# Raw weights as single blocks in one ring of six, pooled tiles in the same ring, and the sixth pair of gates ahead of the first `w_pool` products

## The chip, the core and the metric

The kernel runs on one core of one Trainium2 chip. The core has a matrix engine (TensorE, PE in the profile), a vector engine (VectorE, DVE), a scalar engine (ScalarE, ACT), GpSimd (POOL) and an engine that only issues transfers (SyncE, SP); each works through its own list of instructions in order, and they wait for each other by semaphores. The metric is the device time of one execution in microseconds, as the median of several runs.

## What is computed

One layer of a hybrid block on 1024 tokens of width 1024, in float32. Cut to what matters here:

```python
proj = x @ w_in                    # q | f | i | og | pool_v | gate_a | gate_b
a = hgrn2(q, f, i)                 # 8 heads, per-head RMS norm, * sigmoid(og)
a = a @ w_a
b = per_group(causal_mean(pool_v) - pool_v) @ w_pool[g] * pool_scale   # 4 groups
mix = (sigmoid(gate_a) * a + sigmoid(gate_b) * b) @ w_out
x = LN(alpha * x + mix)
x = LN(alpha * x + square(relu(x @ w_up)) @ w_down)
```

## The kernel before

**Precision and products.** Every float32 operand is split into a high and a low part (`split`, L116: a cast on ScalarE, L118, and a subtraction on VectorE, L119), and a product is three passes on TensorE: high by high (L201), high by low (L203), low by high (L204). One product (`prod`) runs over four blocks of 128 rows and so has twelve matmuls of 128x512 into one PSUM bank. Most matrix products are done in Winograd's form: a pair (`pair`, L263) takes four blocks of weights b11, b12, b21, b22 (512 rows by 128 columns each, for two columns of the output) and makes seven products p1 to p7 instead of eight. Between them it needs differences of blocks on VectorE (t1 to t4), copies of a bank out of PSUM (ScalarE, L271), and additions to those copies (VectorE, L275). p1, p6, p5 and p3 go one after the other onto one bank `a`, p7 and p4 onto `z`, p2 onto `c`; each next product on a bank has to wait until the last result has been copied or added.

**What follows what.** After the first matrix products (values of all heads) eight heads follow, with two halves of 512 tokens each (`hgrn`). Behind a half head come other pairs, as `EXTRAS` says: pooled groups, pairs of gates (`gates(0)` to `gates(7)`, called the first to eighth pair), sums of head outputs (`o_sums`), and the products with `w_pool` (`pool_products(g)`, L105 to L107). At the end of each half head stand the output matmuls (L915, L918), their squares on ScalarE (L923), a load of another activation table, a root (L924), a reciprocal on VectorE (L925), four scalings (L928), four transposes on TensorE (L931). The gates' sigmoid (L696) needs the other activation table again. Then come the pairs of `w_a`, `w_out` and the first norm, sixteen pairs of `w_up` (`units`), and `w_down`.

**The order.** The program is written in this order with some priorities (`tc.high_priority`); a scheduler then makes each engine's list from it with its own model of time, and the pools' rings decide which tile waits for whose release. TensorE takes its list in order, and so do ScalarE, VectorE and the transfers' queue on SP: an instruction that waits holds all behind it on the same engine.

**Raw weights.** `raw_tile` (L206) holds two blocks side by side (b11 and b12, or b21 and b22), from a ring of two; `w_blocks` (L209) loads a pair's blocks with two transfers of 512 KB where its two columns lie side by side, and with four of 256 KB otherwise. The differences t have a ring of two of their own (`w_diff`, L239). Pairs that run alone take their products in the order p1, p2, p6, p7, p5, p4, p3; two pairs that run interleaved (`twin`) in the order p1, p2, p7, p4, p6, p5, p3. The pairs of `w_up` take turns between the ring of two and two tiles of another pool.

**Products with `w_pool`.** `pool_products` (L708) loads `w_pool[g]` into a raw tile and splits it into the rings `q` and `f`; the pooled tiles (`pod`, two for each half of the tokens) are loaded into the rings `og`, `v`, `q`, `f` in turn, which the heads use too, and split into the ring `w` of ten tiles. The gates' results that they are multiplied with (L729) are loaded into the same four rings.

Of the kernel before, what the change touches and what calls it, by code (L numbers as in the profile page):

```python
# [16 lines left out]
P = 128  # L17
# [15 lines left out]
PRIO = 60  # L33
# [10 lines left out]
def tile_hybrid_block(  # L44
# [160 lines left out]

    def raw_tile():  # L206
        return wq.tile([P, CH, 2, P], F32, tag="raw", name=nm("raw"), bufs=2)

    def w_blocks(src, c1, c2, tile_of=raw_tile):  # L209

        raw = tile_of(), tile_of()

        def load(*which):
            for kh in range(2):
                rows_of = src[kh * HALF : (kh + 1) * HALF, :].rearrange("(k p) c -> p k c", p=P)
                if c2 == c1 + P and len(which) == 2:
                    done = nc.sync.dma_start(
                        out=raw[kh].rearrange("p k n c -> p k (n c)"), in_=rows_of[:, :, c1 : c1 + 2 * P]
                    )
                else:  # L220
                    for n in which:
                        c = (c1, c2)[n]
                        done = nc.sync.dma_start(out=raw[kh][:, :, n], in_=rows_of[:, :, c : c + P])
            return done

        return raw, load

    def loaded_blocks(*args):
        raw, load = w_blocks(*args)
        load(0, 1)  # L230
        return raw

# [29 lines left out]

    def pair(raw, rooms, takes, pz_tag="pj", twin=False, pc_tag="pj"):  # L263


        b11, b12, b21, b22 = raw if len(raw) == 4 else (raw[kh][:, :, n] for kh in range(2) for n in range(2))
        c, ps = {}, {}
# [46 lines left out]
        def p6(w):  # L314
            prod(ps["a"], w, "s2", False)
            with tc.high_priority(PRIO):
                c[21] = copied(rooms[1], ps["a"])
                if twin:
                    takes[2](added(c[21], ps["z"]))

        def p4(w):
            prod(ps["z"], w, "a22", False)
            if not twin:
                with tc.high_priority(PRIO):
                    takes[2](added(c[21], ps["z"]))

# [75 lines left out]
    with tc.tile_pool(name="xr", bufs=8, side="right", reuse_waits="tile") as xr:  # L402
# [42 lines left out]
        def raw_tile_rows():  # L445
            return [raw_tile().rearrange("p k n c -> p (k n c)").rearrange("p (k c) -> p k c", c=HALF) for _ in range(2)]

# [137 lines left out]
    def raw_rows(src, k2, cc):  # L585

        raw = raw_tile().rearrange("p k n c -> p (k n c)").rearrange("p (k c) -> p k c", c=HALF)
        rows_of = src[k2 * P : (k2 + 2) * P, cc * HALF : (cc + 1) * HALF].rearrange("(k p) c -> p k c", p=P)
        nc.sync.dma_start(out=raw, in_=rows_of)
        return raw  # L590
# [27 lines left out]
    with tc.tile_pool(name="tmp", bufs=1, side="right", reuse_waits="tile") as tmp:  # L618
# [89 lines left out]
        def pool_products(g):  # L708
# [97 lines left out]
        def hgrn(h, u, ft, q, v, og, state):  # L806
# [138 lines left out]
        nxt = head_inputs(0, (None, None, "p6", None, None))  # L945
        output_gates(0)
# [54 lines left out]
        def a_pair(p):  # L1001
            raw = loaded_blocks(w_a, 2 * p * P, (2 * p + 1) * P, raw_tile if p % 2 else mg_raw)
            room = mg_tile("room", 4)
            takes = [gated(2 * p + i, u, p < 2) for u in range(2) for i in range(2)]
            return pair(raw, (c_tile, room, room), takes, "hg", True)

# [75 lines left out]
    with tc.tile_pool(name="wo", bufs=1, side="right", reuse_waits="tile") as mp:  # L1082
        st1 = [None] * 8
        g1, b1 = ln_params(lambda: f(act_tile()).rearrange("p a b -> p (a b)"), ln1_g, ln1_b)
        for k2 in range(0, KT, 2):
            raw = raw_rows(w_out, k2, 1)
            for k in range(2):
                n = len(wo)
                out_row(raw[:, k], (
                    (lambda: (row_tile(), row_tile())) if n < 10 else  # L1090
# [45 lines left out]
    with tc.tile_pool(name="up", bufs=1, side="right", reuse_waits="tile") as up:  # L1136
# [15 lines left out]
        def units(i, raw):  # L1152
# [27 lines left out]

            return pair(raw, (c_tile,) * 3, (take(0), last, take(2), take(3)), "hg", i < 2, "tr" if i == 2 else "pj")

        def up_blocks(i):
            return w_blocks(w_up, i * 2 * P, i * 2 * P + P, up_raw_tile if i % 2 else raw_tile)

        blocks = [up_blocks(i) for i in range(2)]
        for _, load in blocks:
            load(0, 1)
        pairs = [units(i, raw) for i, (raw, _) in enumerate(blocks)]
        run(pairs[0][1:2])  # L1190
# [20 lines left out]
        for i in range(3, NP):  # L1211
            raw, load = up_blocks(i)
            w_load = load(0, 1)
            if i == NP - 2:
                for part in down_rows(0, ws0):
                    part(w_load)
            run(units(i, raw))
# [184 lines left out]
```

## Time and profile before

| | us |
|---|---|
| median of three runs | 1461.98 (1461.56 to 1463.47) |
| the profiled execution | 1460.19 |
| its span, first to last instruction | 1458.5 |
| TensorE busy | 1436.4 |
| VectorE busy | 1141.6 |
| ScalarE busy | 758.3 |

The times in the profile are those of one execution. "Busy" is the union of an engine's instructions; "idle before" is the time that an engine stood ahead of an instruction, with what ended it behind an arrow. Lines (L123) are those of the kernel; tiles are named output first (`w<-raw` is a split of raw weights). A group with `x12` has twelve instructions. The granted clock is the share of full speed at which TensorE was clocked.

### The profile page before, as it was taken

The numbers are of one execution on the slowest core, as the hardware profiler recorded it, in microseconds if no ns is written. First come the engines' busy times: TensorE is split into PE (matmuls) and PEld (weight loads), VectorE is DVE, ScalarE is ACT, GpSimd is POOL, SyncE is SP. The second block draws the span as 40 slices with busy tenths as digits, with TensorE's granted clock in tenths as the row PEclk, the third lists the DMA queues.
The fourth block names the chain that finished last, engine by engine and source line by source line (L and its number), as shares of the span: only waits on it lengthen the run. The fifth ranks groups of instructions, "written<-read, shape, count | busy, mean of one in ns | idle before, by whom it ended". The sixth has DMA issues, their size and how long they took to land.

```text
span 1458.5 us, 20662 instructions
## 1 busy us (share of the span) xinstructions
PE 1436.4 (98%) x7377; PEld 1187.9 (81%) x7377; DVE 1141.6 (78%) x1838; ACT 758.3 (52%) x1383; POOL 58.6 (4%) x244
## 2 busy tenths in 40 slices
PE   8999999999999998999999999999999999999997
PEld 7888888888888886788888878888888888888886
DVE  5967989899898885768985597666666787777977
ACT  5445565666656655556542376555555443333535
POOL 0001001001000010000002100000000100000000
PEclk9999999999999999999999999999999999999999
DMA  7232233323234447897672225444474874445322
GB/s 253 70 126 87 85 98 101 109 75 114 90 99 138 152 132 249 301 299 241 223 247 99 73 94 195 159 146 144 152 261 149 275 260 150 153 141 163 130 73 116
DMA packets 160615, 226.82 MB, mean 156 GB/s; under 512 B 11232, under 2 KB 84480, under 8 KB 160512
## 3 DMA queue, kind: packets, MB, share of 16 engines
q1 hardware_dynamic: 158576, 218.93, 44.7%
q0 software_dynamic: 1152, 4.19, 0.8%
q10 hardware_dynamic: 784, 2.38, 0.5%
q8 instruction: 58, 0.95, 0.3%
q14 instruction: 45, 0.37, 0.1%
HBM read 154.16 MB, written 71.30 MB: 155 GB/s over the span
## 4 chain that ended last, share of the span: by engine, by line
PE 94%; DVE 3%; DMA 1%; ACT 1%; issue 0%; SPq 0%; DVEq 0%
PE ps_pj L201 16%; PE ps_pj L203 16%; PE ps_pj L204 16%; PE ps_pj L1283 4%; PE ps_pj L1285 4%; PE ps_pj L1284 4%; PE ps_pj L106 3%; PE ps_pj L107 3%; PE ps_pj L105 2%; PE ps_tr L1285 1%; PE ps_tr L1283 1%; PE ps_tr L1284 1%; PE ps_sc L201 1%; PE ps_sc L203 1%; PE ps_sc L204 1%; PE ps_hg L203 1%
## 5 line engine op out<-in xcount | busy, mean ns | idle before, releaser
L201 PE MATMUL ps_pj<-act,w 128*128 128x512 f32 x1068 | 421.6, 395 | 0.4 <-ACT act L123 0.2
L203 PE MATMUL ps_pj<-act,w 128*128 128x512 f32 x1068 | 415.1, 390 | 0.5 <-DVE act L124 0.5
L204 PE MATMUL ps_pj<-act,w 128*128 128x512 f32 x1068 | 414.1, 390 | 0.0
L201 PEld LDWEIGHTS ps_pj<-act,w 128*128 128x128 f32 x1068 | 200.6, 188 | 42.8 <-ACT act L123 0.6
L204 PEld LDWEIGHTS ps_pj<-act,w 128*128 128x128 f32 x1068 | 200.5, 188 | 42.3
L203 PEld LDWEIGHTS ps_pj<-act,w 128*128 128x128 f32 x1068 | 200.6, 188 | 40.6 <-DVE act L124 0.9
L118 ACT CAST w<-t 128x512 fp32r<-128x512 f32 x170 | 104.7, 620 | 105.0 <-PE ps_pj L203 53.8
L118 ACT CAST w<-raw 128x512 fp32r<-128x512 f32 x143 | 88.2, 620 | 117.3 <-PE ps_pj L203 62.5
L119 DVE TENSOR_TENSOR w<-raw,w 128x512 fp32r<-128x512 f32 x143 | 99.8, 702 | 55.2 <-ACT w L118 53.9
L119 DVE TENSOR_TENSOR w<-t,w 128x512 fp32r<-128x512 f32 x170 | 115.9, 685 | 29.6 <-ACT w L118 29.4
L1245 ACT CAST act<-act 128x1024 fp32r<-128x1024 f32 x66 | 66.9, 1050 | 107.9 <-issue 35.0
L1246 DVE TENSOR_TENSOR act<-act,act 128x1024 fp32r<-128x1024 f32 x66 | 79.3, 1220 | 18.5 <-ACT act L1245 15.8
L1285 PE MATMUL ps_pj<-act,act 128*128 128x512 f32 x240 | 92.9, 389 | 0.0
L1284 PE MATMUL ps_pj<-act,act 128*128 128x512 f32 x240 | 92.9, 389 | 0.0
L1283 PE MATMUL ps_pj<-act,act 128*128 128x512 f32 x240 | 92.4, 389 | 0.0
L275 DVE TENSOR_TENSOR c<-c,ps_pj 128x512 f32<-128x512 f32 x95 | 64.5, 681 | 18.0 <-PE ps_pj L204 13.4
L271 ACT COPY c<-ps_pj 128x512 f32<-128x512 f32 x96 | 55.2, 582 | 12.8 <-PE ps_pj L204 12.8
L817 DVE RECIPROCAL tC<-tA 128x128 f32<-128x128 f32 x64 | 54.1, 904 | 0.0
L1284 PEld LDWEIGHTS ps_pj<-act,act 128*128 128x128 f32 x240 | 45.1, 188 | 9.4
L1285 PEld LDWEIGHTS ps_pj<-act,act 128*128 128x128 f32 x240 | 45.1, 188 | 9.4
L1283 PEld LDWEIGHTS ps_pj<-act,act 128*128 128x128 f32 x240 | 45.1, 188 | 9.3
L241 DVE TENSOR_TENSOR t<-raw,raw 128x512 f32<-128x512 f32 x43 | 29.6, 689 | 21.9 <-DMA raw<-in_w_in_dram 19.7
(415 smaller groups left out, 2719.8 us busy)
## 6 DMA issues: line engine op xcount, KB each, us to landing
h<-c SPq DMA_DIRECT2D x106, 256.0 KB, 2.1
act<-h SPq DMA_DIRECT2D x78, 256.0 KB, 2.9
raw<-in_w_in_dram SPq DMA_DIRECT2D x64, 256.0 KB, 3.4
draw<-in_w_down_dram SPq DMA_DIRECT2D x16, 1024.0 KB, 7.8
raw<-in_w_up_dram SPq DMA_DIRECT2D x30, 512.0 KB, 4.2
raw<-in_w_in_dram SPq DMA_DIRECT2D x18, 512.0 KB, 4.0
hf<-h SPq DMA_DIRECT2D x34, 256.0 KB, 2.9
c<-o SPq DMA_DIRECT2D x24, 256.0 KB, 3.4
```

What stands on the lines that cost most here:

```text
L118: A.copy(hi, src)
L119: V.tensor_sub(lo, src, f(hi))
L201: PE.matmul(ps, wh[:, k], th, start=first and k == 0, stop=False, skip_group_check=True)
L203: PE.matmul(ps, wh[:, k], tl, start=False, stop=False, skip_group_check=True)
L204: PE.matmul(ps, wl[:, k], th, start=False, stop=k == CH - 1, skip_group_check=True)
L271: A.copy(t, ps)
L275: V.tensor_add(t, t, ps)
L1245: A.copy(hi, src)
L1246: V.tensor_sub(lo, src, f(hi))
L1283: PE.matmul(ps, hh[:, w], wh, start=fresh and n == 0, stop=False, skip_group_check=True)
L1284: PE.matmul(ps, hh[:, w], wl, start=False, stop=False, skip_group_check=True)
L1285: PE.matmul(ps, hl[:, w], wh, start=False, stop=n == M - 1, skip_group_check=True)
```

## The change

Raw weights become single blocks of 128 x 512 (2 KB in each partition) in one ring of six tiles, which also holds the difference t. A pair alone takes five of them, in the order b11, b21, b12, t, b22, each loaded by its own transfer of 256 KB; pairs whose tiles come from another pool keep two wide transfers. All pairs have the product order p1, p2, p7, p4, p6, p5, p3, and the differences are made in place (b12 becomes t1's operand, b21 t4's). The pooled tiles for `w_pool` are loaded into the ring of six. In `EXTRAS` the sixth pair of gates stands ahead of the first products with `w_pool`. The `w_up` pairs from the fourth on all use the ring.

```diff
-    def raw_tile():
-        return wq.tile([P, CH, 2, P], F32, tag="raw", name=nm("raw"), bufs=2)
...
+    def block_tile(shape=(CH, P)):
+        return wq.tile([P, *shape], F32, tag="raw", name=nm("raw"), bufs=6)
+
+    def wide_block(src, kh, c, t):
+        rows_of = src[kh * HALF : (kh + 1) * HALF, :].rearrange("(k p) c -> p k c", p=P)
+        done = nc.sync.dma_start(out=t, in_=rows_of[:, :, c : c + t.shape[2]])
+        return t, done
+
+    def wide_blocks(src, c1, tile_of):
+        raw = [wide_block(src, kh, c1, tile_of().rearrange("p k n c -> p k (n c)"))[0] for kh in range(2)]
+        return [raw[kh][:, :, n * P : (n + 1) * P] for kh in range(2) for n in range(2)]
+
+    def loaded_blocks(src, c1, c2, done=None):
+        raw = {}
+        for i in ((0, 0), (1, 0), (0, 1), "t", (1, 1)):
+            raw[i] = block_tile(), None
+            if i != "t":
+                raw[i] = wide_block(src, i[0], (c1, c2)[i[1]], raw[i][0])
+        if done is not None:
+            done.append(raw[1, 1][1])
+        return [raw[i][0] for i in ((0, 0), (0, 1), (1, 0), (1, 1), "t")]
...
-    def w_diff(a, b):
-        t = wq.tile([P, CH, P], F32, tag="t", name=nm("t"), bufs=2)
-        V.tensor_sub(t, a, b)
-        return t
...
         def t3():
-            c["t"] = w_diff(b22, b12)
+            c["t"] = block_tile() if t is None else t
+            V.tensor_sub(c["t"], b22, b12)
             return w_part(c["t"])
-        def t2():
-            if not twin:
-                V.tensor_add(c["t"], c["t"], b11)
-            return w_part(c["t"])
-
         def t4():
-            if not twin:
-                V.tensor_sub(c["t"], b21, c["t"])
-                return w_part(c["t"])
-            V.tensor_add(c["t"], c["t"], b11)
+            V.tensor_sub(b12, b12, b11)
+            V.tensor_sub(c["t"], b22, b12)
             V.tensor_sub(b21, b21, c["t"])
             return w_part(b21)
+        def t2():
+            return w_part(c["t"])
+
         def t1():
-            return w_part(w_diff(b12, b11))
+            return w_part(b12)
...
-        return (
-            ((t0,), ((t0, p1),)),
-            ((b_21,), ((b_21, p2),)),
-            *(
-                (((t3,), ((t3, p7),)), ((t4,), ((t4, p4),)), ((t2,), ((t2, p6),)), ((t1,), ((t1, p5),)))
-                if twin
-                else (((t3, t2), ((t2, p6), (t3, p7))), ((t1, t4), ((t1, p5), (t4, p4))))
-            ),
-            ((b_22,), ((b_22, p3),)),
+        return tuple(
+            ((operand,), ((operand, product),))
+            for operand, product in ((t0, p1), (b_21, p2), (t3, p7), (t4, p4), (t2, p6), (t1, p5), (b_22, p3))
         )
...
-            raw = raw_tile().rearrange("p k n c -> p (k n c)")[:, : 2 * 2 * P].rearrange("p (k c) -> p k c", c=2 * P)
+            raw = block_tile((2, 2 * P))
             nc.sync.dma_start(out=raw, in_=w_pool[g].rearrange("(k p) c -> p k c", p=P))
...
-                pl = [split(loaded(pod[2 * g + i][u], room), row_tile) for i in range(2)]
+                pl = [split(loaded(pod[2 * g + i][u], lambda: block_tile((HALF,))), row_tile) for i in range(2)]
...
         EXTRAS[7, 1] = (
-            ("gates", 4), ("o_sums", 2), ("pool_products", 0), ("gates", 5), ("pool_products", 1), ("gates", 6), ("pool_products", 2), ("pool_products", 3), ("gates", 7),
+            ("gates", 4), ("o_sums", 2), ("gates", 5), ("pool_products", 0), ("pool_products", 1), ("gates", 6),
+            ("pool_products", 2), ("pool_products", 3), ("gates", 7),
         )
...
-            raw = loaded_blocks(w_a, 2 * p * P, (2 * p + 1) * P, raw_tile if p % 2 else mg_raw)
+            cols = 2 * p * P, (2 * p + 1) * P
+            raw = loaded_blocks(w_a, *cols) if p % 2 else wide_blocks(w_a, cols[0], mg_raw)
...
-        blocks = [up_blocks(i) for i in range(2)]
-        for _, load in blocks:
-            load(0, 1)
-        pairs = [units(i, raw) for i, (raw, _) in enumerate(blocks)]
+        blocks = loaded_blocks(w_up, 0, P), wide_blocks(w_up, 2 * P, up_raw_tile)
+        pairs = [units(i, raw) for i, raw in enumerate(blocks)]
...
         for i in range(3, NP):
-            raw, load = up_blocks(i)
-            w_load = load(0, 1)
+            done = []
+            raw = loaded_blocks(w_up, i * 2 * P, i * 2 * P + P, done)
```

The places that load rows of `x`'s values and of `w_out` through the ring (`raw_tile_rows`, `raw_rows`) take one tile for each row block instead of half a tile.

More of the change, by code (lines that the diff above doesn't have):

```diff
@@ L261, in c_late, with pair @@
         return c_tile(False)
-    def pair(raw, rooms, takes, pz_tag="pj", twin=False, pc_tag="pj"):
-        b11, b12, b21, b22 = raw if len(raw) == 4 else (raw[kh][:, :, n] for kh in range(2) for n in range(2))
+    def pair(raw, rooms, takes, pz_tag="pj", pc_tag="pj"):
+        b11, b12, b21, b22, t = raw if len(raw) == 5 else (*raw, None)
         c, ps = {}, {}
@@ L317, in p6 @@
                 c[21] = copied(rooms[1], ps["a"])
-                if twin:
-                    takes[2](added(c[21], ps["z"]))
+                takes[2](added(c[21], ps["z"]))
         def p4(w):
             prod(ps["z"], w, "a22", False)
-            if not twin:
-                with tc.high_priority(PRIO):
-                    takes[2](added(c[21], ps["z"]))
         def p5(w):
@@ L445, in raw_tile_rows @@
         def raw_tile_rows():
-            return [raw_tile().rearrange("p k n c -> p (k n c)").rearrange("p (k c) -> p k c", c=HALF) for _ in range(2)]
+            return [block_tile((1, HALF)) for _ in range(4)]
         def load_block(tiles, kh, nh, ks=None):
@@ L585, in raw_rows @@
     def raw_rows(src, k2, cc):
-        raw = raw_tile().rearrange("p k n c -> p (k n c)").rearrange("p (k c) -> p k c", c=HALF)
-        rows_of = src[k2 * P : (k2 + 2) * P, cc * HALF : (cc + 1) * HALF].rearrange("(k p) c -> p k c", p=P)
-        nc.sync.dma_start(out=raw, in_=rows_of)
+        raw = [block_tile((HALF,)) for _ in range(2)]
+        for k in range(2):
+            nc.sync.dma_start(out=raw[k], in_=src[(k2 + k) * P : (k2 + k + 1) * P, cc * HALF : (cc + 1) * HALF])
         return raw
@@ L1001, in a_pair @@
         def a_pair(p):
-            raw = loaded_blocks(w_a, 2 * p * P, (2 * p + 1) * P, raw_tile if p % 2 else mg_raw)
+            cols = 2 * p * P, (2 * p + 1) * P
+            raw = loaded_blocks(w_a, *cols) if p % 2 else wide_blocks(w_a, cols[0], mg_raw)
             room = mg_tile("room", 4)
             takes = [gated(2 * p + i, u, p < 2) for u in range(2) for i in range(2)]
-            return pair(raw, (c_tile, room, room), takes, "hg", True)
+            return pair(raw, (c_tile, room, room), takes, "hg")
         def unpark(*which):
@@ L1179, in last @@
                 put(6, s4)
-            return pair(raw, (c_tile,) * 3, (take(0), last, take(2), take(3)), "hg", i < 2, "tr" if i == 2 else "pj")
-        def up_blocks(i):
-            return w_blocks(w_up, i * 2 * P, i * 2 * P + P, up_raw_tile if i % 2 else raw_tile)
-        blocks = [up_blocks(i) for i in range(2)]
-        for _, load in blocks:
-            load(0, 1)
-        pairs = [units(i, raw) for i, (raw, _) in enumerate(blocks)]
+            return pair(raw, (c_tile,) * 3, (take(0), last, take(2), take(3)), "hg", "tr" if i == 2 else "pj")
+        blocks = loaded_blocks(w_up, 0, P), wide_blocks(w_up, 2 * P, up_raw_tile)
+        pairs = [units(i, raw) for i, raw in enumerate(blocks)]
         run(pairs[0][1:2])
```

24 lines of the change are left out of this document (3 added, 21 removed).

## The prediction

> **What bounds the kernel now.** I read the page first, then what TensorE waited for, then the windows around the largest wait, then the order of time on TensorE and ScalarE there, and last how long the loads take to land.
>
> ```profile
> span 1458.5 us, 20662 instructions
> PE 1436.4 (98%) x7377; PEld 1187.9 (81%) x7377; DVE 1141.6 (78%) x1838; ACT 758.3 (52%) x1383; POOL 58.6 (4%) x244
> PE 94%; DVE 3%; DMA 1%; ACT 1%; issue 0%; SPq 0%; DVEq 0%
> ```
>
> TensorE is busy for 98% of the span and makes 94% of the chain that ended last. The number of its products does not change, so an edit counts only by the stretches in which TensorE stands still or is clocked down. What it waited for:
>
> ```profile
> PE ps_pj L105 <- ACT w L118: 4.7, 1, 4.7
> PE ps_hg L915 <- DVE st L883: 1.2, 1, 1.2
> PE ps_pj L106 <- DVE w L119: 0.8, 1, 0.8
> PE ps_sc L201 <- ACT c L271: 0.5, 1, 0.5
> ```
>
> The first three lie within 20 us, where the last head ends and the first products of `w_pool` (L105, L106) begin. Windows over that place (columns: the window, busy us and count of TensorE, its weight loads, VectorE, ScalarE and GpSimd, then the granted clock, the DMA share and GB/s) and over the rest of the kernel behind it:
>
> ```profile
> 574.98:578.40 3.42, 2.05 (x16) 1.86 (x16) 1.72 (x4) 0.12 (x1) 0.00 (x0) 1.00 0.93 280
> 578.40:581.81 3.41, 0.00 (x0) 0.00 (x0) 1.44 (x3) 1.03 (x8) 0.00 (x0) 1.00 0.93 321
> 581.81:588.64 6.83, 5.75 (x13) 3.92 (x14) 2.69 (x5) 5.99 (x13) 0.00 (x0) 0.50 0.67 217
> 600.00:868.00 268.00, 267.17 (x1206) 220.07 (x1205) 205.13 (x334) 127.17 (x222) 14.78 (x6) 1.00 0.59 198
> 868.00:1050.00 182.00, 181.48 (x801) 150.01 (x800) 122.84 (x190) 106.63 (x182) 0.00 (x0) 1.00 0.46 155
> ```
>
> After 3.4 us without one product the clock stands at half for 6.83 us. In these TensorE works 5.75 us at half speed, which loses 5.75 / 2 = 2.9 us. So this place costs 4.7 + 1.2 + 0.8 + 2.9 = 9.6 us. The last two rows lose about a microsecond in 450. Hence a gain is bounded by some 10 us, and all else can only lose.
>
> **The pace of the parts.** One row after the other on TensorE, and the releaser of the long wait on ScalarE:
>
> ```profile
> 559.97 0.39 PE L201 MATMUL ps_pj<-act,w 128*128 128x512 f32 x1
> 560.20 0.39 PE L203 MATMUL ps_pj<-act,w 128*128 128x512 f32 x1
> ...
> 576.14 0.49 PE L915 MATMUL ps_hg<-v,att 128*128 128x128 f32 x2 [1.21 <-DVE st L883]
> 577.80 0.39 PE L918 MATMUL ps_hg<-st,tA 128*128 128x128 f32 x2
> 582.85 1.22 PE L105 MATMUL ps_pj<-w,q 128*128 128x512 f32 x2 [4.66 <-ACT w L118]
> ```
> ```profile
> 554.06 0.62 ACT L118 CAST q<-raw 128x512 fp32r<-128x512 f32 x1 [3.38 <-DMA raw<-in_w_pool_dram]
> 565.13 0.28 ACT L923 ACTIVATE tH<-ps_hg 128x128 f32<-128x128 f32 x1 [0.93 <-PE ps_hg L918]
> 566.29 1.28 ACT L924 ACT_TABLE_LOAD   x1
> 567.59 0.30 ACT L924 ACTIVATE ss<-ss,eps_rms 128x4 f32<-128x4 f32 x1
> 569.99 1.14 ACT L928 ACTIVATE tH<-ps_hg,ss 128x128 f32<-128x128 f32 x4 [2.10 <-DVE ss L925]
> 571.15 1.28 ACT L696 ACT_TABLE_LOAD   x1
> 574.30 0.60 ACT L696 ACTIVATE c<-ps_pj 128x512 f32<-128x512 f32 x1 [0.33 <-PE ps_pj L204]
> 582.18 0.62 ACT L118 CAST w<-og 128x512 fp32r<-128x512 f32 x1 [2.75 <-DMA og<-po]
> ```
>
> A 128x512 matmul goes every 0.227 us, a product of twelve takes 2.72 us; the eight output matmuls of a half head take 576.14 to 578.0, 1.9 us (seven take 1.5). The squares, table load and root of a half head stand from 565.13 to 567.9, 2.8 us; four scalings take 1.14. The long wait ended with a pooled tile's cast: its load into the `og` ring was late.
>
> **The pooled tiles in the raw ring.** They no longer wait for `og` and `v`, which the last head holds. In the order of the changed kernel's instructions their loads stand behind the splits of the sixth pair, well ahead of their casts. That removes the 4.7 us wait, its half clock and the 0.8.
>
> **The sixth pair ahead.** Its p1, p2 and p7 now lie in the end of the last head; p7 and the preceding product cover the 1.2 us wait at L915. Its loads move ahead on SP's queue, and the loads of `w_pool` fall behind them: `w_pool[0]` waits for the split of the fifth pair's last block, `w_pool[1]` for that of b12 of the sixth. On ScalarE, which works in order, the cast of `w_pool[0]` stands ahead of the squares of the last head's first half, the cast of `w_pool[1]` ahead of those of its second half. The row at 554.06 shows ScalarE standing 3.38 us for just such a cast. How long these loads take:
>
> ```profile
>   ACT q L118: 6.7, 3
> DMA to landing us min/median/max: 3.4/4.1/5.4
> ```
>
> So two new waits arise, with this queued behind them: squares, table, root, scalings, the transposes (L931), then a pooled cast or split, a table load and a sigmoid that frees the PSUM bank of TensorE's next product. Costs of the steps:
>
> ```profile
> L118 ACT CAST w<-raw 128x512 fp32r<-128x512 f32 x143 | 88.2, 620 | 117.3 <-PE ps_pj L203 62.5
> L119 DVE TENSOR_TENSOR w<-raw,w 128x512 fp32r<-128x512 f32 x143 | 99.8, 702 | 55.2 <-ACT w L118 53.9
> L275 DVE TENSOR_TENSOR c<-c,ps_pj 128x512 f32<-128x512 f32 x95 | 64.5, 681 | 18.0 <-PE ps_pj L204 13.4
> L271 ACT COPY c<-ps_pj 128x512 f32<-128x512 f32 x96 | 55.2, 582 | 12.8 <-PE ps_pj L204 12.8
> ```
>
> First half, counted from the end of the fifth pair's p7: two VectorE operations behind the split, about 1.7 us; load 4.1; cast 0.62; squares to root 2.8; reciprocal and first scaling 0.5: the first transpose is ready at 9.7. TensorE meanwhile has 2.72 + 1.5 + 2.72 + 2.72 = 9.7 us of work: nothing lost yet. But the next product, p2, waits for the bank: other three scalings 0.85, cast 0.62, table load 1.28, sigmoid 0.60 = 3.35, and only 0.8 us of transposes cover it: 2.6 lost.
>
> Second half, counted from the end of the fifth pair's p5: addition and split 1.4, load 4.1, cast 0.62, 2.8, 0.5 = 9.4, against 2.72 + 1.9 + 2.72 = 7.3 of work: 2.1 lost. Then again 3.35 up to the bank, less 0.45 of transposes: 2.9. The copy that p4 needs stands behind that sigmoid: 0.58 less one matmul, 0.35. The split of the second pooled tile can use its slot only when p4 has ended: 0.7 lost. Second half: 6.1 us. Together 2.6 + 6.1 = 8.7.
>
> The half clock is not certain. From the end of p3 to the bank TensorE then does 0.45 us of transposes in 5.5 us. The nearest rows are the window with 0.00 busy, after which the clock fell, and the one with 2.05 of 3.42, after which it did not; 0.45 of 5.5 is nearer the first. A window of 3.41 us, at a place that I can't know, lies inside 5.5 us in (5.5 - 3.41) / 3.41 = 6 of 10 cases. The fall costs up to 2.9, some 2.6 as TensorE still stands for a part of it. I take 0.6 x 2.6 = 1.6, with 0 and 2.9 as ends.
> The Trainium skill (TensorE: Matmul & The Clock Gate, "What's actually happening") has half rate after at least one idle window of about 3.4 us, on a free-running window. The trace agrees: 3.41 us without a product, then 0.50. Read strictly, transposes in the window keep it from being idle, the term is 0, and the sum would be 8.7.
>
> **Single blocks in a ring of six.** The same four differences per pair on VectorE, in the same space; the splits read contiguous blocks now, which these rows can't price and whose cover is TensorE's products. 54 more issues on SP, whose queue is not TensorE's bound. Loads of 512-byte rows where they were 1 KB:
>
> ```profile
> raw<-in_w_in_dram SPq DMA_DIRECT2D x64, 256.0 KB, 3.4
> raw<-in_w_up_dram SPq DMA_DIRECT2D x30, 512.0 KB, 4.2
> raw<-in_w_in_dram SPq DMA_DIRECT2D x8, 256.0 KB, 5.7
> ```
>
> (The third row is of 540 to 610 us, with the DMA engines full.) In the `w_up` pairs, whose depth of two pairs is lost, the tightest block has a little over four products, 11 us, between release and use; load, difference and split need 3.4 + 0.7 + 1.3 = 5.4, at worst 7.7. Nothing lost; were it uncovered, 2 us per pair.
>
> **One order of products for all pairs.** p6 and p5 now follow each other on one bank. Where the scheduler found no other product between them, TensorE waits for a copy: once in the `w_a` pairs, with a cast ahead of it, (0.62 - 0.45) + 0.58 less 0.23 cover, plus hops, 0.7 lost. At the start of the `w_up` pairs the reverse: two products on bank `sc` with three matmuls between them have eleven in the new order, and the wait of 0.5 goes. Net +0.2.
>
> **The sum.** 8.7 + 1.6 - 9.6 + 0.2 = +0.9 us. The profiled execution took 1460.19 us, 1.7 more than its span; it becomes 1461.1, and the median of the runs shown, 1461.98, becomes 1462.9. What a measurement can tell from no change is 0.2%, 2.9 us.
>
> **The rivals.**
> Faster: the loads of `w_pool` land before the squares are due. For: VectorE, on which their releases hang, is at 78% only. Against: released 1.4 us behind p5's end, `w_pool[1]` would have to land in 2.6 us, and the shortest of four took 3.4. Then the first half loses 0.7; the second 0.8 before its transposes (3.5 for squares to scaling, less 2.72) and 2.9 + 0.35 + 0.7 behind them: 5.5 in all, no half clock, 5.5 - 9.6 + 0.2 = -3.9: 1458.1. It decides from the point at which `w_pool[1]` lands within 4.0 us of p5's end, so that its cast is done when the output matmuls are (2.72 + 1.9 = 4.6).
> Slower: the wait in front of the squares takes the place of the removed one and grows. The block loads land after 5.7 instead of 3.4 (+1.9 in the first half, as the split waits behind a difference that needs one), `w_pool` after 5.4 (+1.3), and the clock falls (2.9): 8.7 + 1.9 + 1.3 + 2.9 - 9.6 + 0.2 = +5.4: 1467.4. For: DMA share 0.93 in both windows ahead of 581.81.
> The change doesn't do what it says: the pooled casts stay the last to arrive. Against: their loads are issued behind the sixth pair's splits, 5 us or more ahead of their casts. Then 4.7 stays and the squares add 2.6: about +3, 1465.
>
> **How the numbers follow.** Forecast 0.45; faster 0.20; the slower wait 0.28; the pooled casts 0.07. Faster by over 0.2%: 0.20; within: 0.45; slower: 0.35. The likeliest one's own range is 1460.5 to 1464.8. The whole range reaches to both rivals and a little past them for the unknown hops: 1457.5 to 1468.5.
>
> **What would show it.** TensorE's waits at L105 on the pooled cast and at L915 gone; ScalarE idle ahead of the cast of `w_pool[1]` for 2 us or more, released by its load; TensorE waiting at the transposes and then on ScalarE's sigmoid; the granted clock tells of the half rate. Wrong if the stretch from the last head to the last product of `w_pool` has no wait over 1 us, or if waits of that size stand in the `w_up` pairs.

## The result, and the profile after

The changed kernel takes 1467.68 us, median of five runs (1466.61 to 1470.18), against 1462.53 for the kernel before on the same chip (1461.56 to 1463.47): a ratio of 1.0033, with a 95% interval of 1.0021 to 1.0045. By the ratio that is 4.8 us slower, 3.1 to 6.6 by its interval; the two medians lie 5.2 apart. The profiled execution took 1467.09.

Its page, and what TensorE waited for (in total, how often, the longest, us):

```profile
span 1465.4 us, 20846 instructions
PE 1441.8 (98%) x7377; PEld 1190.9 (81%) x7377; DVE 1138.6 (78%) x1838; ACT 757.9 (52%) x1383; POOL 56.7 (4%) x244
PE 90%; DVE 4%; DMA 3%; ACT 2%; issue 1%; SPq 0%; DVEq 0%; ACTq 0%
```
```profile
PE ps_pj L201 <- ACT c L676: 2.1, 1, 2.1
PE ps_pj L105 <- ACT c L676: 2.1, 1, 2.1
PE ps_pj L457 <- ACT act L123: 2.0, 1, 2.0
...
PE ps_tr L911 <- ACT tH L908: 1.4, 2, 1.1
PE sc L878 <- ACT c L676: 1.0, 1, 1.0
PE ps_pj L201 <- ACT act L123: 1.0, 1, 1.0
PE ps_hg L204 <- DVE w L119: 0.9, 1, 0.9
```

The two waits that the change was to remove, on the pooled tile's cast (4.7) and on `st` (1.2), are gone. Seven other lines stand here, all but one on ScalarE (the line left out is a wait of 1.7 us that both kernels have at their start). L676 is the gates' sigmoid (before L696), L903 to L911 are squares to transposes (before L923 to L931), L457 is the first product of the kernel (before L477).

The place of the last head. First ScalarE (start, us, instruction, idle time ahead of it and its releaser), then windows with the granted clock (columns as in the prediction):

```profile
567.26 0.62 ACT L118 CAST q<-raw 128x512 fp32r<-128x512 f32 x1 [3.01 <-DMA raw<-in_w_pool_dram]
567.78 0.27 ACT L903 ACTIVATE tH<-ps_hg 128x128 f32<-128x128 f32 x1
...
573.74 0.60 ACT L676 ACTIVATE c<-ps_pj 128x512 f32<-128x512 f32 x1
...
589.39 0.62 ACT L118 CAST q<-raw 128x512 fp32r<-128x512 f32 x1 [1.19 <-DMA raw<-in_w_pool_dram]
589.92 0.27 ACT L903 ACTIVATE tH<-ps_hg 128x128 f32<-128x128 f32 x1
...
595.88 0.60 ACT L676 ACTIVATE c<-ps_pj 128x512 f32<-128x512 f32 x1
```
```profile
570.79:574.20 3.41, 1.14 (x8) 0.80 (x7) 0.69 (x1) 3.38 (x7) 0.00 (x0) 1.00 0.20 74
574.20:577.62 3.42, 3.23 (x8) 2.56 (x9) 1.77 (x3) 2.00 (x5) 0.00 (x0) 0.50 0.24 79
591.27:594.68 3.41, 2.09 (x9) 1.04 (x7) 0.38 (x2) 3.14 (x8) 0.00 (x0) 1.00 0.82 266
594.68:601.51 6.83, 4.99 (x12) 3.83 (x13) 3.83 (x6) 2.26 (x3) 0.00 (x0) 0.50 0.64 200
```

Both casts of `w_pool` wait for their loads ahead of the squares, as forecast, and the clock falls behind both halves, not behind one.

The start of the kernel, which the prediction did not look at: the changed kernel, then the kernel before (ScalarE, and the first product on TensorE).

```profile
6.87 0.62 ACT L118 CAST w<-b 128x512 fp32r<-128x512 f32 x1 [1.79 <-DMA b<-in_w_in_dram]
9.82 1.14 ACT L118 CAST w<-b 128x512 fp32r<-128x512 f32 x2 [2.33 <-DMA b<-in_w_in_dram]
10.87 0.21 ACT L401 ACTIVATE e<-e 128x16 f32<-128x16 f32 x1
10.98 1.05 ACT L123 CAST act<-ps_tr 128x512 fp32r<-128x512 f32 x2
...
11.60 0.50 PE L457 MATMUL ps_pj<-w,act 128*128 128x512 f32 x1 [1.97 <-ACT act L123]
```
```profile
7.04 0.62 ACT L118 CAST w<-b 128x512 fp32r<-128x512 f32 x1 [1.86 <-DMA b<-in_w_in_dram]
7.56 0.58 ACT L123 CAST act<-ps_tr 128x512 fp32r<-128x512 f32 x1
10.59 0.62 ACT L118 CAST w<-b 128x512 fp32r<-128x512 f32 x1 [2.45 <-DMA b<-in_w_in_dram]
...
10.13 0.48 PE L477 MATMUL ps_pj<-w,act 128*128 128x512 f32 x1
```

In the kernel before, ScalarE casts the first part of x (L123) at 7.56 and only then waits for the third weight row. In the changed kernel the third and fourth rows stand ahead of it, and the third lands only at 9.8, so the cast that the first product needs starts at 10.98.

To compare stretches I take the same TensorE work in each kernel: the time between two products, less what the matmuls started in it take at full clock and undisturbed (0.227 us for 128x512 and 0.11 for 128x128, from the rows; smaller ones 0.03 to 0.06). What is left, the loss, is waits, half clock and the small gaps around them. Stretches are given by TensorE's work in us from its first product on. The start also holds what lies ahead of that product, from the first matmul at 1.65 us on; it is "up to 40 us" in the expectations. The second profile of before is that of the last experiment; what the table leaves out differs by less than 0.5 us.

| loss, us | before | before, 2nd profile | changed |
|---|---|---|---|
| start, 0 to 38 | 6.3 | 6.1 | 7.0 |
| 38 to 455 | 1.0 | 2.1 | 0.7 |
| last heads but one, 455 to 552 | -0.5 | -0.5 | 2.1 |
| last head and `w_pool`, 552 to 640 | 11.7 | 14.5 | 12.0 |
| `w_a` pairs, 640 to 700 | 0.1 | 0.5 | 2.5 |
| `w_up` start, 835 to 875 | 2.1 | 2.1 | 2.9 |
| `w_up` pairs, 875 to 1282 | 0.1 | 0.1 | 0.4 |

### The profile page after: what moved, and what is told of

Read it like the earlier page. It is cut to its first block, busy times and chain, and to the rows that moved or that the text cites. A ratio compares the mean times of both kernels' runs of the same rounds, so it can differ in the third digit from the quotient of the medians.

```text
span 1465.4 us, 20846 instructions
## 1 busy us (share of the span) xinstructions
PE 1441.8 (98%) x7377; PEld 1190.9 (81%) x7377; DVE 1138.6 (78%) x1838; ACT 757.9 (52%) x1383; POOL 56.7 (4%) x244
## 4 chain that ended last, share of the span: by engine, by line
PE 90%; DVE 4%; DMA 3%; ACT 2%; issue 1%; SPq 0%; DVEq 0%; ACTq 0%
PE ps_pj L201 16%; PE ps_pj L203 15%; PE ps_pj L204 15%; PE ps_pj L1261 4%; PE ps_pj L1260 4%; PE ps_pj L1262 4%; PE ps_pj L105 3%; PE ps_pj L106 2%; PE ps_pj L107 2%; PE ps_tr L1262 1%; PE ps_tr L1261 1%; PE ps_tr L1260 1%; DMA raw<-in_w_in_dram 1%; PE ps_hg L204 1%; PE ps_sc L201 1%; PE ps_sc L204 1%
## 5 line engine op out<-in xcount | busy, mean ns | idle before, releaser
L118 ACT CAST w<-raw 128x512 fp32r<-128x512 f32 x327 | 202.0, 622 | 278.0 <-PE ps_pj L203 184.5
L119 DVE TENSOR_TENSOR w<-raw,w 128x512 fp32r<-128x512 f32 x327 | 222.6, 687 | 97.2 <-ACT w L118 94.9
L1223 DVE TENSOR_TENSOR act<-act,act 128x1024 fp32r<-128x1024 f32 x66 | 79.4, 1220 | 14.8 <-ACT act L1222 14.7
L273 DVE TENSOR_TENSOR raw<-raw,raw 128x512 f32<-128x512 f32 x43 | 29.6, 689 | 19.7 <-DMA raw<-in_w_in_dram 17.6
L1131 ACT ACTIVATE c<-c 128x512 f32<-128x512 f32 x61 | 38.7, 634 | 1.5
L1130 ACT ACTIVATE c<-c 128x512 f32<-128x512 f32 x46 | 29.1, 633 | 15.0 <-DVE c L268 15.0
```

The source lines that it names most:

```text
L118: A.copy(hi, src)
L119: V.tensor_sub(lo, src, f(hi))
L1223: V.tensor_sub(lo, src, f(hi))
```

## The experiments

Theory A: a cast that waits for a load holds up ScalarE, and with it what TensorE needs next, at the start and at both halves of the last head. Theory B: the moved sixth pair is the cost. Theory C: what is gained at the last head comes back behind it. The table has every run (ratios to runs of the kernel before on the same chip; losses of one profile each, as above; "heads" is 455 to 552).

| run | median us | ratio, 95% interval | start | heads | last head, `w_pool` | `w_a` |
|---|---|---|---|---|---|---|
| changed | 1467.68 | 1.0033 (1.0021 to 1.0045) | 7.0 | 2.1 | 12.0 | 2.5 |
| e1 pair behind | 1467.61 | 1.0028 (1.0017 to 1.0039) | 10.1 | 2.6 | 10.3 | 1.9 |
| e2 pair ahead only | 1468.44 | 1.0031 (1.0019 to 1.0043) | 5.9 | -0.5 | 18.1 | 2.3 |
| e3 pooled tiles in old rings | 1471.04 | 1.0052 (1.0040 to 1.0064) | 11.2 | 2.3 | 13.0 | 3.9 |
| e4 pooled tiles in raw ring only | 1464.13 | 1.0003 (0.9994 to 1.0012) | 5.5 | -0.5 | 12.6 | 3.2 |
| e5 early `w_pool` split | 1465.56 | 1.0019 (1.0010 to 1.0028) | 10.7 | 2.6 | 8.1 | 2.6 |
| e6 one order only | 1464.77 | 1.0011 (1.0002 to 1.0020) | 6.3 | 2.7 | 11.6 | 2.0 |
| e7 ring, old order | 1473.57 | 1.0075 (1.0061 to 1.0090) | 7.3 | -0.3 | 18.5 | 4.3 |
| e8 start pinned | 1463.88 | 1.0000 (0.9991 to 1.0009) | 7.7 | 2.2 | 10.8 | 2.6 |
| e9 both remedies | 1461.23 | 0.9986 (0.9978 to 0.9995) | 4.6 | 2.9 | 8.0 | 2.1 |
| e10 before, late first cast | 1464.51 | 1.0010 (1.0001 to 1.0019) | 7.8 | -0.5 | 12.8 | 0.3 |
| e11 p2 in another bank | 1455.98 | 0.9948 (0.9936 to 0.9960) | 4.6 | 3.4 | 2.4 | 2.2 |
| e12 before again | 1463.65 | 1.0006 (0.9998 to 1.0015) | 6.1 | -0.5 | 14.5 | 0.5 |

**Is it the moved pair?** e1 is the changed kernel with the old order of extras:

```diff
-            ("gates", 4), ("o_sums", 2), ("gates", 5), ("pool_products", 0), ("pool_products", 1), ("gates", 6),
-            ("pool_products", 2), ("pool_products", 3), ("gates", 7),
+            ("gates", 4), ("o_sums", 2), ("pool_products", 0), ("gates", 5), ("pool_products", 1), ("gates", 6), ("pool_products", 2), ("pool_products", 3), ("gates", 7),
```

> Two theories of where the 4.8 us come from. Theory A: the stretch of the last head gives its gain back to new waits and half clock there (loss in the stretch 12.6 us against 10.8), and the rest, about 5 us, is lost outside it, in the parts that the block ring and the single order of products reordered. Theory B: the sixth pair ahead of the first products of w_pool is the whole cost, and the ring costs nothing. Here the sixth pair stands behind the first products of w_pool again, all else is as changed: w_pool[1] is cast seven operations ahead of the second half's squares and should have landed. A: the loss in the stretch falls to about 7 us, the 5 us outside it stay: about 1462.5 us, ratio to before 0.999 to 1.001. B: the pooled tiles' gain is kept in full and nothing else is lost: 1455 us, ratio 0.995.

1467.61: neither. The stretch lost only 1.7 us less (10.3, where A had about 7), and the profile lost 10.1 us at the start. B falls, since without the moved pair the time is the same; A's 1462.5 us was too low as well.

e2 is the kernel before with that line changed the other way, and nothing else.

> The kernel before with the sixth pair ahead of the first products of w_pool and nothing else: old rings, old orders of products, pooled tiles in the old rings. The cast of w_pool[0] now stands behind the first half's squares, w_pool[1] behind the second's; a pooled tile's cast stands ahead of the second half's squares. A: no wait of 1 us or more outside the last head's stretch; inside it three more products cover the pooled tile's load, so the 4.7 us wait shrinks to at most 2: 1455 to 1460 us. B: the moved pair costs what it costs in the changed kernel: 1466 us or more.

1468.44, as B says in size, and against A: with the old rings the moved pair costs 4 to 6 us in the stretch (18.1 against 14.5 and 11.7), in the changed kernel 1.7. So its price hangs on what else is changed: the rings, or the order of products. e7 below points to the order, for with the ring of six, the old order and the pair ahead the stretch loses 18.5, as much as here. No run has the ring, the old order and the pair behind, so this is not shown.

**The pooled tiles.** e3 puts them back into the old rings of the changed kernel; e4 does this part alone in the kernel before:

```diff
-                pl = [split(loaded(pod[2 * g + i][u], lambda: block_tile((HALF,))), row_tile) for i in range(2)]
+                pl = [split(loaded(pod[2 * g + i][u], room), row_tile) for i in range(2)]
```
```diff
-                pl = [split(loaded(pod[2 * g + i][u], room), row_tile) for i in range(2)]
+                two = raw_tile().rearrange("p k n c -> p (k n c)")
+                pl = [split(loaded(pod[2 * g + i][u], lambda: two[:, i * HALF : (i + 1) * HALF]), row_tile) for i in range(2)]
```

> The changed kernel with the pooled tiles loaded into the old rings (og, v) again. The cast of w_pool[0] still stands ahead of the first half's squares; w_pool[1] is cast behind the second half's scalings. A: the first half loses as in the changed kernel (2.5 us of waits, half clock 1.6), the second loses less than the 3.2 us of waits and 2.5 of half clock seen there unless the og tile is late: 1464 us, 3 to 4 us under the changed kernel, and the losses outside the stretch stay as they are. B: as the pair is still ahead, and a pooled tile is late besides: 1468 us or more.

> The kernel before with the pooled tiles loaded into its raw ring of two (two pooled tiles in one raw tile), nothing else: old orders, sixth pair behind. Both theories: the wait of 4.7 us on the pooled tile, the 0.8 us behind it and the half clock of 2.9 go. A: nothing is lost outside the stretch; a new wait for the bank behind the second half's sigmoid may take 1 to 3 us: 1455 to 1458 us. B: 1454 us. If it is not below 1459, both are wrong about what the pooled tile's wait was worth.

e3: 1471.04, slower than the changed kernel, where A had 1464 and B 1468 or more. Of the 6.5 us by which its profile is longer 4.2 lie at the start, which the edit does not touch, 1.0 at the last head and 1.4 in the `w_a` pairs. By the ratios (1.0052 and 1.0033) the old rings cost 2.8 us here, with intervals that overlap a little: the ring of six is worth having for the pooled tiles, not by much. e4: 1464.13, no change, where both theories had 5 us less. The wait of 4.7 us and the half clock did go, yet the time did not. Windows of e4, then of the kernel before:

```profile
580.00:600.00 20.00, 17.54 (x85) 14.04 (x84) 13.86 (x25) 10.96 (x28) 0.00 (x0) 1.00 0.81 279
...
620.00:640.00 20.00, 17.99 (x74) 13.13 (x73) 9.11 (x14) 7.77 (x14) 0.00 (x0) 1.00 0.84 285
640.00:660.00 20.00, 16.88 (x67) 11.58 (x66) 16.26 (x27) 12.97 (x23) 0.00 (x0) 1.00 0.87 306
```
```profile
580.00:600.00 20.00, 16.27 (x60) 12.31 (x61) 13.29 (x22) 8.85 (x18) 0.00 (x0) 0.83 0.79 266
...
620.00:640.00 20.00, 20.00 (x90) 16.56 (x89) 10.37 (x17) 9.56 (x17) 0.00 (x0) 1.00 0.90 296
640.00:660.00 20.00, 19.85 (x88) 15.99 (x87) 17.42 (x29) 13.72 (x26) 0.00 (x0) 1.00 0.85 281
```

In e4 TensorE starts 85 matmuls instead of 60 from 580 to 600, and 74 and 67 instead of 90 and 88 from 620 to 660. The loss left the last head (11.1 to 3.6 us, up to 600 us of work) and came back with the next products of `w_pool` and the next pairs (0.5 to 9.0, up to 640). Casts of raw tiles there, 616 to 660, in e4 and in the kernel before (busy us and mean ns, then the idle time ahead of them and what ended it):

```profile
L118 ACT CAST w<-raw 128x512 fp32r<-128x512 f32 x12 | 7.4, 618 | 10.4 <-DMA raw<-po 7.7 <-DMA raw<-in_w_in_dram 2.2 <-PE ps_pj L107 0.6
```
```profile
L118 ACT CAST w<-raw 128x512 fp32r<-128x512 f32 x6 | 3.7, 621 | 1.5 <-PE ps_pj L106 1.5
```

The kernel before has its pooled casts in two other groups, and none of these waits for a load either:

```profile
L118 ACT CAST w<-og 128x512 fp32r<-128x512 f32 x4 | 2.5, 624 | 1.8 <-issue 1.0 <-PE ps_pj L203 0.5 <-PE ps_pj L106 0.2
L118 ACT CAST w<-v 128x512 fp32r<-128x512 f32 x4 | 2.5, 622 | 7.1 <-PE ps_pj L203 3.7 <-issue 2.4 <-ACT c L696 0.9
```

In e4 ScalarE waits 9.9 us for loads into the raw ring of two, which pooled tiles and blocks now share. The gain came back behind the place, as theory C says. That it does so because the ring has two tiles is not shown: e7 below loses as much there with six.

**The casts of `w_pool`.** e5 is the changed kernel with load and split of `w_pool[0]` and `w_pool[1]` written ahead of the sixth pair (`pool_weights` is the first half of `pool_products`, cut off):

```diff
-            ("gates", 4), ("o_sums", 2), ("gates", 5), ("pool_products", 0), ("pool_products", 1), ("gates", 6),
+            ("gates", 4), ("o_sums", 2), ("pool_weights", 0), ("pool_weights", 1), ("gates", 5), ("pool_products", 0), ("pool_products", 1), ("gates", 6),
```

> The changed kernel with the loads and splits of w_pool[0] and w_pool[1] written ahead of the sixth pair, so that their casts stand on ScalarE well ahead of the squares of the last head's first half. Theory A (a cast that waits for a load holds up in-order ScalarE, and with it what TensorE needs): the squares of the first half start 2.5 us earlier, so its waits of 0.37 and 2.09 us and its half clock of 1.6 us go; those of the second half start 0.6 us earlier: 4.7 us less loss in the stretch, 1463 us. Theory C (between the last head and the end of the w_a pairs the transfers run at 300 to 400 GB/s, and a stall that is removed comes back behind it): the loss of the stretch falls as much, and 3 us or more of it come back up to the end of the w_a pairs: 1466 us or more.

The stretch lost 8.1 instead of 12.0 us, 3.9 less (4.7 forecast), and the `w_a` pairs as much as in the changed kernel (2.6): with the ring of six and the one order nothing comes back, against C. The median is 1465.56, between the two forecasts: it fell by 2.1 only, and the profile shows 10.7 us lost at the start. Its windows there:

```profile
8.06:11.48 3.42, 1.47 (x10) 1.00 (x9) 1.20 (x5) 1.22 (x3) 0.31 (x1) 1.00 1.05 399
11.48:18.30 6.82, 5.64 (x13) 4.46 (x14) 4.73 (x12) 5.61 (x13) 0.00 (x0) 0.50 1.05 389
```

Behind the late first product the clock is at half for 6.8 us: 13 matmuls in them.

**Order or ring?** e6 is the kernel before with the one order (`twin` true for all pairs), e7 the changed kernel with the old two-step order.

> The kernel before with the one order of products for all pairs and nothing else: old ring of two wide tiles, pooled tiles in the old rings, sixth pair behind. If the order makes the losses that all kernels with ring and order together show and none of the old ones does (1.1 us at 464 to 484 us, 1 us at 535 to 555, 0.8 us at the start of the w_up pairs), they are here: 2 to 3 us outside the last head's stretch, 1465 us. If the ring makes them, the losses outside the stretch are those of before within 0.5 us: 1462 to 1463.5 us.

> The changed kernel with the old two-step order of products in all pairs that had it, everything else as changed (ring of six, pooled tiles in it, sixth pair ahead). If the order makes the losses at 464 to 484, 535 to 555 and at the start of the w_up pairs, they go: 2 to 3 us less outside the stretch, about 1465 us. If the ring makes them, they stay. The start of the kernel keeps its later first product in both cases (w cast of three rows ahead of the first cast of x), 1 to 5 us.

The heads answer without doubt: -0.3 to -0.5 us in all kernels with the old order, ring or not, 2.1 to 3.4 in all with the one order, though not at the same products: e6 loses 1.8 of them at 535 to 552, the changed kernel 1.0 at 464 to 475. Some of it is earned back earlier (38 to 455: 1.0 and 2.1 in the two profiles of before, 0.2 in e6). The `w_up` start goes with the ring: 2.1 to 2.2 in all kernels without it, 2.9 with it. e6 as a whole is 1.0011, 1.6 us, as forecast: its heads and `w_a` pairs lose more than that, and the rest wins some of it back. e7 came out at 1473.57, 8 us off what I had for it: with the old order the changed kernel loses 18.5 us at the last head and 4.3 in the `w_a` pairs, so this change needs the one order. Some 9 of the 18.5 lie between 600 and 640 us of work, where e4 lost its 9.0, and the longest wait there goes back to a load into the ring of six, late like those of e4 (VectorE in e7):

```profile
650.88 0.69 DVE L273 TENSOR_TENSOR raw<-raw,raw 128x512 f32<-128x512 f32 x1 [4.70 <-DMA raw<-in_w_in_dram]
```

e4 and e7 share the old order and the pooled tiles in the raw ring, not the ring's size.

**The start.** e8 is the changed kernel with three casts held behind the first cast of x on ScalarE; `made_first` is that cast:

```diff
-        w = parts(b11)
+        w = parts(b11[:1])
+        with tc.issue_after(made_first["a11"]):
+            w += parts(b11[1:])
```

> The changed kernel with the casts of the second to fourth weight row of the first product kept behind the first cast of x on ScalarE, as the kernel before has the first of them; the order on TensorE is otherwise nearly the same. In the three profiles with the block ring these casts, which wait for their loads, stood ahead of the cast that the first product needs: TensorE waited 1.1 to 2.0 us for it, and the loss up to 40 us was 7.0, 10.1 and 11.2 us against 6.3, 5.9 and 5.5 of the old ring. Theory A: the loss up to 40 us falls to about 6: 1 to 4 us less, 1464 to 1466.5 us. Rival: the start differs only by the moment at which the loads land and by where the clock's windows lie, and nothing changes beyond a microsecond: 1467 us or more.

1463.88, a ratio of 1.0000 (0.9991 to 1.0009): by the runs on the same chip all of the slowing is gone, with a last head nearly as in the changed kernel (10.8 against 12.0). ScalarE in e8:

```profile
4.51 0.62 ACT L118 CAST w<-b 128x512 fp32r<-128x512 f32 x1 [0.94 <-DMA b<-in_w_in_dram]
8.86 0.22 ACT L402 ACTIVATE e<-e 128x16 f32<-128x16 f32 x1 [3.73 <-DVE e L401]
8.98 1.05 ACT L123 CAST act<-ps_tr 128x512 fp32r<-128x512 f32 x2
```

The cast of x starts at 8.98 instead of 10.98. One profile alone would mislead: e8's, its slowest run, lost 7.7 us at the start, with 2.5 of waiting for a load of x and half clock for 3.4, the changed kernel's 7.0. Over all profiles the five kernels with the changed start lost 7.0, 7.3, 10.1, 10.7 and 11.2 us, mean 9.3 (the three large ones with the clock at half for 6.8 us); five with the old start 5.5 to 6.3, mean 6.0; the three pinned ones 7.7, 4.6 and 4.6, mean 5.6.

e10 is the reverse: the kernel before, with the first cast of x put behind that of the third weight row (`with tc.issue_after(made_hi["rows"])` around `first_tokens("a11", ...)`).

> The reverse test: the kernel before with the cast of the third weight row put ahead of the first cast of x on ScalarE, as the changed kernel has it; the order on TensorE is otherwise nearly the same. Theory A: the first product waits 1 to 2 us more for that cast and in most runs the clock falls behind it: the loss up to 40 us rises from 6 to between 7 and 11 us, 1464.5 to 1468 us. Rival (the start is no cause): 1463 to 1464 us.

1464.51, at the lower edge of theory A: 1.0010 (1.0001 to 1.0019). What TensorE waited for at its first product there:

```profile
PE ps_pj L477 <- ACT act L123: 1.4, 1, 1.4
```

The wait appears, the start loses 7.8 us instead of 6.2, and the median rises by 1.2. That is a third of the 3.8 that e8 took off; the edit moves the third row's cast alone, where the changed kernel has the fourth ahead too. The clock did not fall at the start of its profile, and hardly in its other runs: the mean granted clock was 0.996 or 0.997 in eleven of twelve, as in the kernel before, and 0.993 in one (1469.34 us). A's fall of the clock in most runs did not come. In e5 the profiled run is one of three in eleven with 0.993, the others have 0.995 or 0.996. So profiles with the fall are probably over-represented in the mean of 9.3.

**Both, and a step further.** e9 joins e5 and e8; e11 gives p2 of the sixth pair a bank of the transposes' tag (`pc_tag="tr" if j == 5 else "pj"` in `gates`).

> The changed kernel with both remedies: w_pool[0] and w_pool[1] split ahead of the sixth pair, and the casts at the start kept behind the first cast of x. If the two costs are independent, the medians add: the start alone took 3.8 us off the changed kernel, the early split 2.1 us with 4.0 less loss in the stretch: 1460 to 1462 us, ratio to before 0.998 to 0.999. If the transfers bound the part behind the last head (theory C), 1463 us or more.

> As the run with both remedies, and the product p2 of the sixth pair in a bank of the transposes' tag, so that it needs no bank that the sigmoid behind the second half's squares frees; that sigmoid moves ahead of the squares on ScalarE and p2 lies among the transposes. If the wait for the bank and the second half clock (2.1 and 2.5 us in the changed kernel) hang on that sigmoid, both go: 3 to 5 us less than the run with both remedies, 1456 to 1459 us. If they come back behind the place as with the pooled tiles in the old ring, no less than 1460 us.

e9: 1461.23, as forecast, 6.4 under the changed kernel, where 3.8 and 2.1 add to 5.9. e11: 1455.98, 0.9948 of the kernel before, at the fast end of its forecast and the fastest of all. Its page and the place of the last head:

```profile
span 1453.4 us, 20852 instructions
PE 1434.7 (99%) x7377; PEld 1187.0 (82%) x7377; DVE 1138.8 (78%) x1838; ACT 755.7 (52%) x1383; POOL 57.1 (4%) x244
```
```profile
582.96 0.59 ACT L679 ACTIVATE c<-ps_pj 128x512 f32<-128x512 f32 x1
583.45 0.58 ACT L265 COPY c<-ps_pj 128x512 f32<-128x512 f32 x1
584.45 0.28 ACT L915 ACTIVATE tH<-ps_hg 128x128 f32<-128x128 f32 x1 [0.42 <-PE ps_hg L910]
...
587.86 0.33 PE L923 MATMUL ps_tr<-ident,tH 128*128 128x128 f32 x1 [0.72 <-ACT tH L920]
587.95 0.48 PE L202 MATMUL ps_tr<-act,w 128*128 128x512 f32 x1
...
590.77 0.49 PE L923 MATMUL ps_tr<-ident,tH 128*128 128x128 f32 x3
```

The sigmoid (L679 here) runs ahead of the squares, p2 lies between the first transpose and the others, and the clock stays full from the start to the last products: the stretch loses 2.4 us.

e12 was the kernel before once more.

> The kernel before once more, for a second profile of it: its profiled execution took 1460.2 us, 3 us less than the median of its runs. If that execution was a lucky one, this one shows where the 3 us lie: at the start (loss up to 40 us above 6.3) or around the last head (loss there above 11.7, clock halved for longer than 6.83 us). If the w_a pairs lose more than 0.5 us here, the 2.4 us that they lose more in the changed kernel are chance too.

1463.65. Its profiled execution took 4.6 us more than the first, and 2.8 of them lie at the last head, though its clock was at half for only 3.4 us there; the start agrees (6.1 and 6.3). So the first profile was lucky there, by waits and not by its clock. The `w_a` pairs reach 0.5, not 2.5: that difference is hardly chance.

## Where the prediction was right, and where it was wrong

The forecast was 1462.9, no change that a measurement can tell; the measured 1467.68 is slower by more than that, inside the whole range and outside the likeliest one's own (1460.5 to 1464.8). The whole range reaches that far only for the slower rival, whose 14.8 us of new losses at the last head did not come (10.0, as worked out below): that it holds the time is luck. The likeliest account was right about the last head and missed the time elsewhere. Step by step:

- **What bounds the kernel, and the old place at 9.6 us**: right in kind. The stretch of the kernel before loses 11.7 and 14.5 us in two profiles.
- **The pooled tiles in the raw ring**: the wait on them and that at L915 went, as said. That all of 4.7 + 0.8 + 2.9 is thereby won was not asked of what follows: e4 won it at the place and lost it again within 80 us.
- **The new waits, 8.7**: the right waits, at the right places. Measured were 0.4 at the first half's transposes (forecast 0), 2.1 at p2's bank (2.6), 1.1 at the second half's transposes (2.1), 2.1 at the bank (2.9), and 0.2 behind it (1.05 for the copy and the split): 5.9. `w_pool[0]` and `w_pool[1]` landed 2.6 and 3.0 us after their issue, sooner than the 4.1 taken. ScalarE waited 1.19 for the second, where 2 or more was forecast, and 3.01 for the first, which was issued late: the split that releases it stood behind a difference that waited for a block's load on VectorE, and that load took 4.8 us, not 3.4:

```profile
562.57 0.69 DVE L273 TENSOR_TENSOR raw<-raw,raw 128x512 f32<-128x512 f32 x1 [2.91 <-DMA raw<-in_w_in_dram]
```

- **The half clock, 1.6**: too small. It fell twice. In the windows above, 3.2 and 5.0 us of work at half speed lose 1.6 and 2.5. The strict reading, with a term of 0, is refuted: the window from 591.27 had nine matmuls and the clock still fell.
- **The stretch together**: 5.9 + 4.1 = 10.0 measured, 10.3 forecast. Two errors of opposite sign made it right, which is luck. The table's loss of 12.0 has 2 us more than these terms, as the kernel before has (11.7 against 9.6).
- **One order of products for all pairs, net +0.2; single blocks, "nothing lost"**: this step failed: +0.2 was forecast, and the order alone costs some 1.6 us in the runs (e6). It priced the operations and transfers of a pair, and the places where one bank follows itself. It did not ask where the scheduler puts other instructions once tiles, transfers and order differ. The start, in which the prediction has no term at all, costs 3.3 us by the means of five profiles each; the heads cost 2.6 and win 0.9 back; the `w_a` pairs 2.2 instead of 0.7; the `w_up` start loses 0.75 instead of winning 0.5. That the `w_up` pairs behind it lose nothing was right (0.1 to 0.4 us).
- **The slower rival** met the time (1467.4) by another mechanism. Of its late loads the block's came true (4.8 us), those of `w_pool` did not; together the new waits are smaller than forecast, not larger, and removing those of the first half (e5) leaves more than half of the slowing. Its fall of the clock came true.

By these means and the profiles, with before at the mean of its two, the parts add to 3.3 - 0.9 + 2.6 - 1.1 + 2.2 + 0.75 = 7 us, against 4.8 (3.1 to 6.6) by the ratio. With the changed kernel's own start (7.0, so 0.8 and not 3.3) they add to 4.4, near the 4.6 by which its profiled execution is longer (1467.09, against a mean of 1462.5 for the two of before). So the start's share lies between some 1 us and the 3.8 that e8 took off, and the split is not known better than 2 to 3 us. Shown by an edit of their own are the start (e8, and in part e10), the casts of `w_pool` (e5), the bank (e11), the heads (e6, e7). Open is the cause in the `w_a` pairs: every kernel with any part of the change loses 1.9 to 4.3 us there, and the two of before and e10 at most 0.5. In the changed kernel the largest wait there stands behind the cast of an operand whose load was late:

```profile
686.82 1.14 ACT L123 CAST act<-c 128x512 fp32r<-128x512 f32 x2 [2.92 <-DMA c<-o]
```

What delays that load was not tried.

## What to carry to other kernels

Where a scheduler makes the lists, a change of tiles moves instructions in places that the diff does not name: compare each in-order engine's list over the whole program, and look first for a cast that waits for a load and now stands ahead of work the busiest engine needs. A wait removed is worth what the next bound leaves of it, so ask which ring or bank the freed work meets next: the pooled tiles' wait came back with the old order of products, in the ring of two (e4), and as large a loss stood there with the old order in the ring of six (e7); with the ring of six and the one order it did not come back. Where starts and clock vary from run to run, one profile of each kernel does not split a difference of 5 us; medians of edits that undo one suspected cost do it better.

## What the runs showed of the hardware

The clock needs no idle window to fall. With the granted clock's own grid of 3.41 us, worked out from clock records and matmul starts of the profiles, all 35 falls in the fourteen profiles, 14 of them at a kernel's end, followed windows with 0 to 1.36 us of matmuls (those started in the window, at their full pace), while of some 5900 windows that kept full clock none had less than 1.22. From half clock it rose behind windows with 1.36 us or more and stayed behind those with 1.36 or less. So in these profiles the boundary lies near 1.3 us in 3.41, some 40% of a window. The Trainium skill (TensorE: Matmul & The Clock Gate, "What's actually happening") has the fall after at least one idle window; the length of its window agrees, the condition does not, and the measurement decides.

Where that grid lies varies: the clock rose first between 4.7 and 7.6 us into the span, though the first matmul started at 1.65 or 1.66 us in every profile. So the same wait costs half clock in one execution and none in the next: the three starts with 10.1 to 11.2 us of loss had it, and those with 7.0 and 7.3 had the wait alone.
